# Attention's transfers on other queues, and the last combination ahead of the z gate

## The chip, the cores and the metric

The kernel runs on one core of a Trainium2 chip. Five engines work side by side, each in the order of its own instruction queue: TensorE (PE) multiplies matrices, VectorE (DVE), ScalarE (ACT) and GpSimd (POOL) work on tiles, and SyncE (SP) here only issues transfers. GpSimd issues transfers too. A transfer runs on the core's 16 DMA engines once its issuing queue has come to it and its waits are fulfilled. The metric is the time of one execution in device microseconds, the median over runs.

## The reference, cut to what matters

One step of a hybrid decoder with one layer: an input projection, an attention head group beside a state-space head group, an output projection, cross attention and an MLP. The change lies in the prompt's attention (2048 positions, 8 heads of 64): three dilated branches, whose outputs are averaged with the softmax of their log-sum-exps.

```python
DILATED_BRANCHES = ((128, 1), (512, 4), (2048, 16))

def combine_branches(outs, lses):
    w = jax.nn.softmax(jnp.stack(lses, axis=0), axis=0)
    return jnp.sum(w[..., None] * jnp.stack(outs, axis=0), axis=0)
```

Right behind it the kernel computes the other head group's gate, SiLU(z) times the scan's output, where z is a column block of the input projection.

## The kernel before

The prompt's attention is `phase_att`. It runs from about 655 to 963 us of the span. Its work is cut into four groups `g` of two heads, and each group into 24 steps: three branches `b`, eight pairs of query blocks each. A step issues the scores of its own pair (L975, TensorE), their masked maximum (L985, VectorE) and exponential (L987, ScalarE), the transposition of the pair before (L995, TensorE; L1000, VectorE), and the product with the values of the pair before that (L1008, TensorE). Then comes whatever has been put down for that step in the table `todo` by `at(step, function)`. So the order of the program is written out by hand: what a step's list says stands on the engines' queues behind the step's own instructions.

Put down there are:

- `first(g+1)`, at step 24g + 13: `load_qk` (L915) loads the next group's queries and keys, high and low parts, four transfers of 1 MB (L920), into the shared buffers `g_b` 0 to 3.
- `turned`, six casts per group on GpSimd (`by_residue`, L934), one per step from the group's first. They reorder queries and keys by residue for the second and third branches. The last two, `t_q`, read the queries' buffers again.
- `value`, the value loads (L941, L944, L947) on SyncE.
- `combine(g)` (L1020), which weighs and adds the three branch outputs of group g while the next group runs. `gather` collects maxima and sums by way of the array `s_stat` into `t_R`; `least` takes the least shift and the differences; `exps` the exponentials and the sum of the denominators; `coef` a reciprocal on VectorE (L1074) and a product (L1075), stores the coefficients to `s_coef` (L1076) and loads them back, broadcast over partitions, as `t_cf` (L1084). `chunk(c)`, four times, multiplies the outputs with them (L1093) and adds (L1096), on GpSimd; `store(c)` (L1103) writes the result to `s_att`. The tuple `times` (L1106) says how many steps into the next group each part stands; for the last group (g == 3) there is no next one, and the parts stand among the z gate's work.

For g == 3 the short operations run on VectorE, and each chunk has two multiplications and one addition on VectorE and one each on GpSimd.

The following stage, `Trunk.group`, is advanced step by step from attention's last steps by `next(fill)`. Its z gate takes the residual stream (L1383, loaded by GpSimd into `g_b` 0 to 7), multiplies it by the z columns (L1441, L1442, L1444), and in `gated` (L1571) evacuates each result: a product on VectorE (L1575), a tanh on ScalarE (L1576) and a product on GpSimd (L1577). `W.ahead` has GpSimd scale the next weights (L1274); ScalarE and VectorE split them into a high and a low part (L1230, L1231). The first two blocks of z are evacuated while attention's last steps end; the other two follow, and then the memory's keys, whose operand `load_memory` loads from GpSimd (L1629).

Of the kernel before, what the change touches and what calls it, by code (L numbers as in the profile page):

```python
# [10 lines left out]
F32 = mybir.dt.float32  # L11
# [7 lines left out]
P = 128  # L19
D = 1024  # L20
T = 2048
# [880 lines left out]
def phase_att(E, trunk):  # L902


    nc, tc = E.nc, E.tc
    with ExitStack() as ctx:
# [6 lines left out]
        s_att = E.s_att  # L913

        def load_qk(g):  # L915

            tiles = []
            for i, src in enumerate((E.s_qh, E.s_ql, E.s_kh, E.s_kl)):
                t = trunk.lend(i, T)
                nc.gpsimd.dma_start(t, src[g])  # L920
                tiles.append(t)
            return tiles

# [96 lines left out]
        def combine(g, stats, outs):  # L1020

            R = sp.tile([NS, 3, 2, P], F32, name="t_R", bufs=1)
            mn = sp.tile([NS, P], F32, name="t_mn", bufs=1)
            ex = sp.tile([NS, 3, P], F32, name="t_ex", bufs=1)
            dd = sp.tile([NS, 2, P], F32, name="t_dd", bufs=1)
            queue = nc.sync
            short = nc.vector if g == 3 else nc.gpsimd

            def nat(b, s):
                if b == 0:  # L1030
                    return R[:, 0, s, :]
                return R[:, b, s, :].rearrange("p (r a) -> p a r", r=4 if b == 1 else 16)

            def like(t, b):
                if b == 0:
                    return t
                return t.rearrange("p (a r) -> p a r", r=4 if b == 1 else 16)

            def gather():
                ps = pp.tile([P, 512], F32, name="t_pst", tag="t_pt", bufs=2)  # L1040
                for s in range(2):
                    for u in range(2):
                        nc.tensor.transpose(ps[:48, (2 * s + u) * P:(2 * s + u + 1) * P], stats[:, s, u, :], E.ident)
                rows = sp.tile([48, 4, P], F32, name="t_rows", bufs=1)
                nc.vector.tensor_copy(rows[:32].rearrange("p s l -> p (s l)"), ps[:32])
                for s in range(4):
                    nc.vector.tensor_copy(rows[32:48, s].rearrange("p (i j m) -> p i j m", i=4, j=4),
                                          ps[32:48, s * P:(s + 1) * P].rearrange("p (j i m) -> p i j m", i=4, j=4))
                dst = E.s_stat[g]
                nc.sync.dma_start(dst[0].rearrange("s r l -> r s l"), rows[0:16])  # L1050
                nc.sync.dma_start(dst[1].rearrange("s (i r) (q a) -> (r q) (s i) a", i=4, q=4),
                                  rows[16:32].rearrange("p s (i a) -> p (s i) a", i=4))
                nc.sync.dma_start(dst[2].rearrange("s i (r m) -> r (s i) m", m=8),
                                  rows[32:48].rearrange("p s (i m) -> p (s i) m", m=8))
                queue.dma_start(R.rearrange("p b s l -> p (b s) l"),
                                dst.rearrange("b (s u) r l -> (u r) (b s) l", s=2))

            def least():
                nc.vector.tensor_tensor(like(mn, 1), like(nat(0, 0), 1), nat(1, 0), op=ALU.min)
                nc.vector.tensor_tensor(like(mn, 2), like(mn, 2), nat(2, 0), op=ALU.min)  # L1060
                for b in range(3):
                    short.tensor_tensor(like(ex[:, b, :], b), like(mn, b), nat(b, 0), op=ALU.subtract)

            def exps():
                nc.scalar.activation(ex, ex, AF.Exp)
                short.tensor_tensor(dd[:, 0, :], ex[:, 0, :], nat(0, 1), op=ALU.mult)
                for b in (1, 2):
                    short.tensor_tensor(like(dd[:, 1, :], b), like(ex[:, b, :], b), nat(b, 1), op=ALU.mult)
                    short.tensor_tensor(dd[:, 0, :], dd[:, 0, :], dd[:, 1, :], op=ALU.add)

            cfs = {}

            def coef():
                nc.vector.reciprocal(dd[:, 0, :], dd[:, 0, :])  # L1074
                short.tensor_tensor(ex, ex, dd[:, 0:1, :].to_broadcast([NS, 3, P]), op=ALU.mult)  # L1075
                queue.dma_start(E.s_coef[g].rearrange("b (r l) -> r b l", l=P), ex)  # L1076
                for c in range(4 if g == 3 else 2):
                    bcast(c)

            def bcast(c):  # L1080
                cf = cfs[c] = sp.tile([P, 3, 512], F32, name="t_cf", tag="t_cf" if c < 2 or g < 3 else "t_o",
                                      bufs=2 if c < 2 or g < 3 else 5)
                for u in range(2):
                    queue.dma_start(cf[64 * u:64 * u + 64],  # L1084
                                    E.s_coef[g].rearrange("b (u t) -> u b t", u=2)[u, None, :, 512 * c:512 * c + 512]
                                    .to_broadcast([64, 3, 512]))

            def chunk(c):
                f = cfs[c].rearrange("p b (j l) -> p b j l", j=4)
                o = [outs[g, b].rearrange("p (j i l) -> p i j l", i=4, j=4)[:, c] for b in range(3)]  # L1090
                for b in range(3):
                    e = nc.vector if g == 3 and b < 2 else nc.gpsimd
                    e.tensor_tensor(o[b], o[b], f[:, b], op=ALU.mult)  # L1093
                for b in (0, 1):
                    e = nc.vector if g == 3 and b < 1 else nc.gpsimd
                    e.tensor_tensor(o[b + 1], o[b + 1], o[b], op=ALU.add)  # L1096
                if c < 2 and g < 3:
                    bcast(c + 2)
                if g == 3:
                    store(c)  # L1100

            def store(c):
                nc.sync.dma_start(s_att[g * P:(g + 1) * P, :T].rearrange("p (j i l) -> p i j l", i=4, j=4)[:, c],  # L1103
                                  outs[g, 2].rearrange("p (j i l) -> p i j l", i=4, j=4)[:, c])

            times = (0, 4, 4, 4, 6, 6, 7, 7) if g == 3 else (0, 3, 4, 5, 7, 8, 9, 10, 17, 17, 17, 17)  # L1106
            return zip(times, (gather, least, exps, coef, *(lambda c=c, f=f: f(c) for f in (chunk, store) for c in range(4))))

        steps = [(g, b, 2 * i) for g in range(4) for b in range(3) for i in range(8)]
        N = len(steps)  # L1110
        st16 = {}
        st, vs, stats, outs, ps, prs, ptb, todo, pos, end = {}, {}, {}, {}, {}, {}, {}, {}, {}, []
# [40 lines left out]
        def first(g):  # L1153
            st[g] = load_qk(g)
# [19 lines left out]
        for g in range(4):  # L1174
            if g < 3:
                at(24 * g + 13, lambda g=g: first(g + 1))
                at(24 * g + 15, lambda g=g: value(g + 1, 0))
                at(24 * g + 17, lambda g=g: value(g + 1, 1))
                at(24 * g + 26, lambda g=g: value(g + 1, 2))
            at(24 * g + 24, lambda g=g: [at(24 * g + 24 + d, f) for d, f in  # L1180
                                         combine(g, stats[g], outs)])
            for k in range(6):
                at(max(24 * g, 2) + k, lambda g=g, k=k: turned(g, k))
# [6 lines left out]
        i, fill = 0, trunk.work  # L1190
# [1190 lines left out]
```

## Time and profile before

| | |
|---|---|
| median of 3 runs | 3525.11 us (3522.56 to 3529.34) |
| profiled execution | 3526.22 us |
| its span | 3524.4 us |
| TensorE busy | 3318.4 us (94%) |
| VectorE, ScalarE, GpSimd busy | 57%, 33%, 37% |
| mean granted TensorE clock | 0.969 of full speed |

The span is what the profile covers of its execution, and each time below is counted from its start. In a timeline a row is a run of instructions of one line on one engine, with its start, its length, what it writes and reads, how many there were, and in brackets for how long the engine stood idle before it and what it then waited for. In a row of windows stand the stretch and its length, the busy time of each engine with the count of instructions, the granted TensorE clock (PEclk, 1.00 is full speed), the busy share of the DMA engines, and what they moved. Its share can come out above 1.

### The profile page before, as it was taken

The numbers are of one execution on the slowest core, as the hardware profiler recorded it, in microseconds if no ns is written. First come the engines' busy times: TensorE is split into PE (matmuls) and PEld (weight loads), VectorE is DVE, ScalarE is ACT, GpSimd is POOL, SyncE is SP. The second block draws the span as 40 slices with busy tenths as digits, with TensorE's granted clock in tenths as the row PEclk, the third lists the DMA queues.
The fourth block names the chain that finished last, engine by engine and source line by source line (L and its number), as shares of the span: only waits on it lengthen the run. The fifth ranks groups of instructions, "written<-read, shape, count | busy, mean of one in ns | idle before, by whom it ended". The sixth has DMA issues, their size and how long they took to land. (4 is left out here: it accounts for less than half of the span.)

```text
span 3524.4 us, 52948 instructions
## 1 busy us (share of the span) xinstructions
PE 3318.4 (94%) x20615; PEld 2945.5 (84%) x20615; DVE 2005.4 (57%) x4068; ACT 1145.6 (33%) x2604; POOL 1306.0 (37%) x1047
## 2 busy tenths in 40 slices
PE   9998988897978999999999999989999999999998
PEld 7998988676767887777776677789888999999998
DVE  4334889876665344567764455564334455555555
ACT  5433333586634333311111111243443311111113
POOL 1114455567633333586611122444224431122113
PEclk9999999898989999999999999999999999999999
DMA  7668333545675121355435533632441222222222
GB/s 207 204 201 237 88 96 94 187 122 161 166 193 145 56 62 40 117 198 195 163 102 183 163 109 98 208 103 61 137 130 33 90 96 78 96 94 92 96 79 97
DMA packets 406365, 447.25 MB, mean 127 GB/s; under 512 B 39868, under 2 KB 338543, under 8 KB 402530
## 3 DMA queue, kind: packets, MB, share of 16 engines
q1 hardware_dynamic: 376066, 382.51, 35.1%
q0 software_dynamic: 30048, 61.35, 6.0%
q8 instruction: 163, 2.67, 0.3%
q14 instruction: 88, 0.72, 0.1%
HBM read 368.33 MB, written 142.44 MB: 145 GB/s over the span
## 5 line engine op out<-in xcount | busy, mean ns | idle before, releaser
L1441 PE MATMUL g_g<-g_b,w_hi 128*128 128x352 f32 (+1 forms) x1760 | 629.5, 359 | 10.1 <-ACT w_hi L1230 8.7
L1442 PE MATMUL g_g<-g_b,w_lo 128*128 128x352 f32 (+1 forms) x1760 | 621.3, 354 | 8.2 <-DVE w_lo L1231 8.1
L1958 POOL TENSOR_TENSOR g_small<-g_small 128x352 f32<-128x352 f32 (+1 forms) x160 | 143.3, 897 | 960.6 <-ACT g_a L1957 960.6
L1231 DVE TENSOR_TENSOR w_lo<-w_raw,w_hi 128x512 fp32r<-128x512 f32 x400 | 345.6, 869 | 193.8 <-ACT w_hi L1230 193.0
L1230 ACT ACTIVATE w_hi<-w_raw 128x512 fp32r<-128x512 f32 x400 | 241.1, 622 | 610.6 <-issue 355.9
L1968 PE MATMUL g_a<-g_a,w_hi 128*128 128x352 f32 (+3 forms) x1076 | 391.3, 364 | 22.3 <-DVE g_a L1978 18.5
L1969 PE MATMUL g_a<-g_a,w_lo 128*128 128x352 f32 (+3 forms) x1076 | 384.8, 358 | 1.9 <-DVE w_lo L1231 1.9
L1970 PE MATMUL g_a<-g_a,w_hi 128*128 128x352 f32 (+3 forms) x1076 | 383.5, 356 | 0.9 <-DVE g_a L1959 0.9
L1441 PEld LDWEIGHTS g_g<-g_b,w_hi 128*128 128x128 f32 x1760 | 335.7, 191 | 56.7 <-ACT w_hi L1230 13.6
L1442 PEld LDWEIGHTS g_g<-g_b,w_lo 128*128 128x128 f32 x1760 | 335.3, 191 | 39.5 <-DVE w_lo L1231 9.9
L1444 PE MATMUL g_g<-g_b,w_hi 128*128 128x352 f32 (+1 forms) x1760 | 366.7, 350 | 0.0
L1978 DVE TENSOR_TENSOR g_a<-g_a,g_a 128x512 f32<-128x512 f32 (+2 forms) x504 | 292.4, 591 | 109.1 <-PE g_a L1970 108.0
L1444 PEld LDWEIGHTS g_g<-g_b,w_hi 128*128 128x128 f32 x1760 | 304.9, 188 | 30.5 <-DMA g_b<-s_xl 0.3
L1957 ACT ACTIVATE g_a<-g_small 128x352 fp32r<-128x352 f32 (+1 forms) x160 | 87.9, 551 | 634.8 <-DVE g_small L1956 634.8
L1956 DVE SCALAR_TENSOR_TENSOR g_small<-g_g,g_rb 128x352 f32<-128x352 f32 (+1 forms) x160 | 94.1, 588 | 316.6 <-PE g_g L1444 285.5
L1968 PEld LDWEIGHTS g_a<-g_a,w_hi 128*128 128x128 f32 x1076 | 202.7, 188 | 71.0 <-DVE g_a L1978 30.6
L1441 PE MATMUL g_g<-g_a,w_hi 128*128 128x352 f32 (+1 forms) x632 | 228.7, 363 | 5.7 <-ACT g_a L1510 4.2
L1442 PE MATMUL g_g<-g_a,w_lo 128*128 128x352 f32 (+1 forms) x632 | 226.3, 359 | 3.1 <-DVE w_lo L1231 2.9
L1970 PEld LDWEIGHTS g_a<-g_a,w_hi 128*128 128x128 f32 x1076 | 203.1, 189 | 23.7 <-DVE g_a L1959 1.3
L1969 PEld LDWEIGHTS g_a<-g_a,w_lo 128*128 128x128 f32 x1076 | 202.8, 188 | 22.5 <-DVE w_lo L1231 2.9
L987 ACT ACTIVATE w_spare<-w_spare,t_stats 128x256 f32<-128x256 f32 (+1 forms) x376 | 168.7, 450 | 74.5 <-DVE t_stats L985 74.3
L1959 DVE TENSOR_TENSOR g_a<-g_small,g_a 128x352 fp32r<-128x352 f32 (+1 forms) x160 | 186.4, 1166 | 2.6 <-POOL g_small L1958 2.4
(468 smaller groups left out, 6988.5 us busy)
## 6 DMA issues: line engine op xcount, KB each, us to landing
w_raw<-in_w_up_dram SPq DMA_DIRECT2D x64, 512.0 KB
w_raw<-in_w_down_dram SPq DMA_DIRECT2D x64, 512.0 KB
out_dram<-in_cache_win_k_dram SPq DMA_DIRECT2D x32, 1022.0 KB
out_dram<-in_cache_win_v_dram SPq DMA_DIRECT2D x32, 1022.0 KB
g_wide<-in_cache_win_k_dram SPq DMA_DIRECT2D x32, 512.0 KB
t_cf<-s_coef SPq DMA_DIRECT2D x32, 384.0 KB
g_spare<-in_cache_win_v_dram SPq DMA_DIRECT2D x48, 256.0 KB
a_xn<-in_x_prompt_dram SPq DMA_DIRECT2D x16, 512.0 KB
```

What stands on the lines that cost most here:

```text
L987: nc.scalar.activation(pr[:, u, :w], pr[:, u, :w], AF.Exp, bias=nm, scale=-1.0, accum_out=stats[:, 1, u, col:col + 1])
L1230: nc.scalar.activation(hi, src, AF.Copy)
L1231: nc.vector.tensor_tensor(lo, src, hi.bitcast(F32), op=ALU.subtract)
L1441: mm(ps[:, :n], hi[:, k], rhs[0][k][:, s], start=first and k == ks[0], stop=False)
L1442: mm(ps[:, :n], lo[:, k], rhs[0][k][:, s], start=False, stop=False)
L1444: mm(ps[:, :n], hi[:, k], rhs[1][k][:, s], start=False, stop=last and k == ks[-1])
L1958: nc.gpsimd.tensor_tensor(t1[:, :k], t1[:, :k], t1[:, :k], op=ALU.mult)
L1959: line.later(3, lambda: nc.vector.tensor_tensor(ul[:, s], t1[:, :k], uh[:, s].bitcast(F32), op=ALU.subtract))
L1968: mm(ps[:, :k], hi[:, j, c], us[f, j, 0][:, s], start=(j == 0), stop=False)
L1969: mm(ps[:, :k], lo[:, j, c], us[f, j, 0][:, s], start=False, stop=False)
L1970: mm(ps[:, :k], hi[:, j, c], us[f, j, 1][:, s], start=False, stop=(j == 1))
L1978: nc.vector.tensor_tensor(xs[m][:, s], xs[m][:, s], ps[:, :k], op=ALU.add)
```

## The change

The four loads of `load_qk` are issued by SyncE and no longer by GpSimd. The store of the coefficients and the loads of `t_cf` are issued by GpSimd and no longer by SyncE, and so are the last group's four stores to `s_att`. For the first three combinations `coef` and the chunks stand one step later; `least`, `exps` and the stores stay where they were. For the last combination `least`, `exps` and `coef` stand two steps earlier, ahead of the first evacuation of the z gate, and the chunks two steps earlier too; attention's last steps end with that, so that `load_memory` is put down one block earlier. From L1026 on, line numbers in the changed kernel are one lower.

```diff
@@ -917,7 +917,7 @@
             tiles = []
             for i, src in enumerate((E.s_qh, E.s_ql, E.s_kh, E.s_kl)):
                 t = trunk.lend(i, T)
-                nc.gpsimd.dma_start(t, src[g])
+                nc.sync.dma_start(t.bitcast(F32), src[g])
                 tiles.append(t)
             return tiles
 
@@ -1023,7 +1023,6 @@
             mn = sp.tile([NS, P], F32, name="t_mn", bufs=1)
             ex = sp.tile([NS, 3, P], F32, name="t_ex", bufs=1)
             dd = sp.tile([NS, 2, P], F32, name="t_dd", bufs=1)
-            queue = nc.sync
             short = nc.vector if g == 3 else nc.gpsimd
 
             def nat(b, s):
@@ -1052,7 +1051,7 @@
                                   rows[16:32].rearrange("p s (i a) -> p (s i) a", i=4))
                 nc.sync.dma_start(dst[2].rearrange("s i (r m) -> r (s i) m", m=8),
                                   rows[32:48].rearrange("p s (i m) -> p (s i) m", m=8))
-                queue.dma_start(R.rearrange("p b s l -> p (b s) l"),
+                nc.sync.dma_start(R.rearrange("p b s l -> p (b s) l"),
                                 dst.rearrange("b (s u) r l -> (u r) (b s) l", s=2))
 
             def least():
@@ -1073,7 +1072,7 @@
             def coef():
                 nc.vector.reciprocal(dd[:, 0, :], dd[:, 0, :])
                 short.tensor_tensor(ex, ex, dd[:, 0:1, :].to_broadcast([NS, 3, P]), op=ALU.mult)
-                queue.dma_start(E.s_coef[g].rearrange("b (r l) -> r b l", l=P), ex)
+                nc.gpsimd.dma_start(E.s_coef[g].rearrange("b (r l) -> r b l", l=P), ex)
                 for c in range(4 if g == 3 else 2):
                     bcast(c)
 
@@ -1081,9 +1080,9 @@
                 cf = cfs[c] = sp.tile([P, 3, 512], F32, name="t_cf", tag="t_cf" if c < 2 or g < 3 else "t_o",
                                       bufs=2 if c < 2 or g < 3 else 5)
                 for u in range(2):
-                    queue.dma_start(cf[64 * u:64 * u + 64],
-                                    E.s_coef[g].rearrange("b (u t) -> u b t", u=2)[u, None, :, 512 * c:512 * c + 512]
-                                    .to_broadcast([64, 3, 512]))
+                    nc.gpsimd.dma_start(cf[64 * u:64 * u + 64],
+                                        E.s_coef[g].rearrange("b (u t) -> u b t", u=2)[u, None, :, 512 * c:512 * c + 512]
+                                        .to_broadcast([64, 3, 512]))
 
             def chunk(c):
                 f = cfs[c].rearrange("p b (j l) -> p b j l", j=4)
@@ -1100,10 +1099,11 @@
                     store(c)
 
             def store(c):
-                nc.sync.dma_start(s_att[g * P:(g + 1) * P, :T].rearrange("p (j i l) -> p i j l", i=4, j=4)[:, c],
-                                  outs[g, 2].rearrange("p (j i l) -> p i j l", i=4, j=4)[:, c])
-
-            times = (0, 4, 4, 4, 6, 6, 7, 7) if g == 3 else (0, 3, 4, 5, 7, 8, 9, 10, 17, 17, 17, 17)
+                queue = nc.gpsimd if g == 3 else nc.sync
+                queue.dma_start(s_att[g * P:(g + 1) * P, :T].rearrange("p (j i l) -> p i j l", i=4, j=4)[:, c],
+                                outs[g, 2].rearrange("p (j i l) -> p i j l", i=4, j=4)[:, c])
+
+            times = (0, 2, 2, 2, 4, 4, 5, 5) if g == 3 else (0, 3, 4, 6, 8, 9, 10, 11, 17, 17, 17, 17)
             return zip(times, (gather, least, exps, coef, *(lambda c=c, f=f: f(c) for f in (chunk, store) for c in range(4))))
 
         steps = [(g, b, 2 * i) for g in range(4) for b in range(3) for i in range(8)]
```

SyncE, at the third group of attention, from the load of its third branch's values to the stores of the combination (`g_b` are the buffers of the next group's queries and keys, `t_v` value tiles). Rows with - stood there before, rows with + stand there now.

```order
 L947 DMA t_v<-s_v 128x2048
-L1076 DMA s_coef_88<-t_ex 32x3x128
-L1084 DMA t_cf<-s_coef_88 64x3x512 x8
+L920 DMA g_b_9688<-s_qh 128x2048
+L920 DMA g_b_9690<-s_ql 128x2048
+L920 DMA g_b_9692<-s_kh 128x2048
+L920 DMA g_b_9694<-s_kl 128x2048
 L941 DMA t_v_9788<-s_v 128x16x128
 L944 DMA t_v<-s_v 32x4x512 x4
 L1103 DMA s_att<-t_o 128x4x128 x4
```

The coefficients' nine transfers have left this place, and the four loads have taken it.

GpSimd at the same place, from the combination's last short product on, before:

```order
-L1075 TENSOR_TENSOR t_ex<-t_ex,t_dd 32x384
-L1093 TENSOR_TENSOR t_o<-t_o,t_cf 128x4x128 x3
-L1096 TENSOR_TENSOR t_o<-t_o 128x4x128 x2
-L1093 TENSOR_TENSOR t_o<-t_o,t_cf 128x4x128 x3
-L1096 TENSOR_TENSOR t_o<-t_o 128x4x128 x2
-L1093 TENSOR_TENSOR t_o<-t_o,t_cf 128x4x128 x3
-L1096 TENSOR_TENSOR t_o<-t_o 128x4x128 x2
-L1093 TENSOR_TENSOR t_o<-t_o,t_cf 128x4x128 x3
-L1096 TENSOR_TENSOR t_o<-t_o 128x4x128 x2
-L920 DMA g_b_9688<-s_qh 128x2048
-L920 DMA g_b_9690<-s_ql 128x2048
```

And now:

```order
+L1074 TENSOR_TENSOR t_ex<-t_ex,t_dd 32x384
+L1075 DMA s_coef_88<-t_ex 32x3x128
+L1083 DMA t_cf<-s_coef_88 64x3x512 x4
+L1092 TENSOR_TENSOR t_o<-t_o,t_cf 128x4x128 x3
+L1095 TENSOR_TENSOR t_o<-t_o 128x4x128 x2
+L1083 DMA t_cf<-s_coef_88 64x3x512 x2
+L1092 TENSOR_TENSOR t_o<-t_o,t_cf 128x4x128 x3
+L1095 TENSOR_TENSOR t_o<-t_o 128x4x128 x2
+L1083 DMA t_cf<-s_coef_88 64x3x512 x2
+L1092 TENSOR_TENSOR t_o<-t_o,t_cf 128x4x128 x3
+L1095 TENSOR_TENSOR t_o<-t_o 128x4x128 x2
```

The store of the coefficients and their first four loads stand between the product and chunk 0, two more loads behind chunk 0 and two behind chunk 1; the loads of queries and keys are gone from the chunks' end.

VectorE at the start of the z gate, before:

```order
L1567 TENSOR_SCALAR g_rbz<-g_rbz 128x1024
L1575 TENSOR_TENSOR g_small<-g_g,g_rbz 128x512
L1515 SCALAR_TENSOR_TENSOR g_a_11346<-g_small,g_a_11346 128x512
L1575 TENSOR_TENSOR g_small<-g_g,g_rbz 128x512
L1059 TENSOR_TENSOR t_mn<-t_R 32x128
L1060 TENSOR_TENSOR t_mn<-t_mn,t_R 32x128
L1062 TENSOR_TENSOR t_ex<-t_mn,t_R 32x128 x3
```

And now, from the reciprocal's product on (the rows of `least` and `exps` stand ahead of these, right behind L1567):

```order
L1074 TENSOR_TENSOR t_ex<-t_ex,t_dd 32x384
L1575 TENSOR_TENSOR g_small<-g_g,g_rbz 128x512
L1515 SCALAR_TENSOR_TENSOR g_a_11346<-g_small,g_a_11346 128x512
L1575 TENSOR_TENSOR g_small<-g_g,g_rbz 128x512
L1092 TENSOR_TENSOR t_o<-t_o,t_cf 128x4x128 x2
L1095 TENSOR_TENSOR t_o<-t_o 128x4x128
L1092 TENSOR_TENSOR t_o<-t_o,t_cf 128x4x128 x2
L1095 TENSOR_TENSOR t_o<-t_o 128x4x128
L1515 SCALAR_TENSOR_TENSOR g_a_11346<-g_small,g_a_11346 128x512
L1231 TENSOR_TENSOR w_lo<-w_raw,w_hi 128x512
```

The whole combination has moved ahead of the gate's first product (L1575), and chunks 0 and 1 (L1092, L1095) ahead of the low half of the next weights (L1231).

## Rows read from the trace of the kernel before

**Rows 1.** Windows of attention groups: length, busy time by engine, PEclk, DMA share, GB/s.
```profile
720.90:797.80 76.90, 67.67 (x762) 54.55 (x761) 56.21 (x255) 59.31 (x224) 52.95 (x39) 0.94 0.56 151
...
sum 229.10, PE 201.95 PEld 163.08 DVE 161.94 ACT 167.47 POOL 161.16; mean PE 67.32 PEld 54.36 DVE 53.98 ACT 55.82 POOL 53.72
```

**Rows 2.** Timeline of TensorE at two group starts: start, us, instruction, idle before.
```profile
797.80 0.48 PE L975 MATMUL t_pss<-g_b,g_b 64*128 64x128 f32 x2 [6.10 <-DMA g_b<-s_kh]
...
876.48 0.47 PE L975 MATMUL t_pss<-g_b,g_b 64*128 64x128 f32 x2 [7.07 <-DMA g_b<-s_kh]
```

**Rows 3.** Timeline of GpSimd, second group, same columns.
```profile
747.46 0.99 POOL L1075 TENSOR_TENSOR t_ex<-t_ex,t_dd 32x384 f32<-32x384 f32 x1
757.41 3.75 POOL L1093 TENSOR_TENSOR t_o<-t_o,t_cf 128x512 f32<-128x512 f32 x3 [8.96 <-DMA t_cf<-s_coef]
...
776.62 3.74 POOL L1093 TENSOR_TENSOR t_o<-t_o,t_cf 128x512 f32<-128x512 f32 x3 [0.22 <-DMA t_cf<-s_coef]
...
782.90 0.60 POOL L920 DMA_DIRECT2D g_b<-s_qh  x1
```

**Rows 4.** Timeline of VectorE, the reciprocal in the fourth group.
```profile
903.65 0.94 DVE L1074 RECIPROCAL t_dd<-t_dd 32x128 f32<-32x128 f32 x1 [4.07 <-POOL t_dd L1069]
```

**Rows 5.** Timeline of SyncE's queue, start of attention and second group.
```profile
640.56 0.37 SPq L577 DMA_DIRECT2D s_y<-s_yg  x1
...
730.17 0.39 SPq L947 DMA_DIRECT2D t_v<-s_v  x1
...
750.01 18.94 SPq L1084 DMA_DIRECT2D t_cf<-s_coef  x8
```

**Rows 6.** Windows of three stretches of transfers.
```profile
752.00:760.00 8.00, 8.00 (x86) 6.61 (x84) 4.33 (x24) 5.27 (x21) 2.58 (x3) 0.84 0.92 189
786.00:798.00 12.00, 5.90 (x72) 4.63 (x70) 5.12 (x31) 7.54 (x32) 6.52 (x2) 0.90 1.10 397
946.00:969.00 23.00, 19.25 (x137) 14.49 (x136) 10.33 (x43) 11.22 (x39) 5.48 (x11) 0.93 1.08 348
```

**Rows 7.** Timeline of TensorE, the first scores.
```profile
657.45 1.67 PE L975 MATMUL t_pss<-g_b,g_b 64*128 64x128 f32 x24
```

**Rows 8.** Timeline of GpSimd, third and fourth groups.
```profile
815.50 1.41 POOL L1062 TENSOR_TENSOR t_ex<-t_mn,t_R 32x128 f32<-32x128 f32 x3 [9.53 <-DVE t_mn L1060]
...
826.79 0.99 POOL L1075 TENSOR_TENSOR t_ex<-t_ex,t_dd 32x384 f32<-32x384 f32 x1
...
871.57 14.40 POOL L934 CAST g_b<-g_b 128x2048 fp32r<-128x2048 f32 x4 [6.83 <-DMA g_b<-s_qh]
885.95 1.89 POOL L1274 TENSOR_TENSOR w_raw<-w_raw,g_gm 128x1024 f32<-128x1024 f32 x1
...
917.65 3.76 POOL L1093 TENSOR_TENSOR t_o<-t_o,t_cf 128x512 f32<-128x512 f32 x3 [9.47 <-DMA t_cf<-s_coef]
...
944.00 0.60 POOL L1383 DMA_DIRECT2D g_b<-s_xh  x1
```

**Rows 9.** Timeline of TensorE, z gate and memory.
```profile
958.83 0.50 PE L1441 MATMUL g_g<-g_b,w_hi 128*128 128x512 f32 x1 [1.39 <-DMA g_b<-s_xh]
...
985.94 0.51 PE L1441 MATMUL g_g<-g_b,w_hi 128*128 128x512 f32 x1 [3.41 <-ACT w_hi L1230]
...
1030.38 0.58 PE L1223 MATMUL g_g<-g_kv,w_hi 128*128 128x256 f32 x1 [3.79 <-DMA g_kv<-s_ml]
```

**Rows 10.** Timeline of VectorE, combination of the last group.
```profile
979.99 0.37 DVE L1059 TENSOR_TENSOR t_mn<-t_R 32x128 f32<-32x128 f32 x1
...
987.51 0.55 DVE L1075 TENSOR_TENSOR t_ex<-t_ex,t_dd 32x384 f32<-32x384 f32 x1
```

**Rows 11.** Timeline of GpSimd, two chunks of the last group.
```profile
1000.40 1.73 POOL L1093 TENSOR_TENSOR t_o<-t_o,t_cf 128x512 f32<-128x512 f32 x1
...
1004.40 1.71 POOL L1093 TENSOR_TENSOR t_o<-t_o,t_cf 128x512 f32<-128x512 f32 x1
```

**Rows 12.** Window of a norm and a pass of the z gate.
```profile
1012.30:1020.00 7.70, 7.51 (x29) 5.11 (x28) 7.63 (x7) 4.85 (x7) 6.31 (x5) 1.00 0.12 35
```

## The prediction

> **What bounds the kernel now.** I read the windows by group first, then TensorE's waits in that stretch, then the timelines of GpSimd and SyncE around each wait. The reader is to see in the windows that the three groups of attention that follow the first take 229.1 us, and that in the first of them TensorE is busy for 67.67 us at a granted clock of 0.94 [rows 1]. That is 63.6 us at full clock; three times that is 191. So 38 us is all that can be won in this stretch: idle time, and the low clock that goes with it.
>
> The waits name the causes. Where a group ends, the first scores of the next wait for its keys, 6.10 and 7.07 us [rows 2]. In GpSimd's timeline the load of the next queries is issued at 782.90, right behind the last addition of the combination, whose first chunk began at 757.41 after 8.96 us of waiting for coefficients [rows 3]. The loads go when GpSimd comes to them, not when their buffers are free: GpSimd's last reader of them, the cast before 747.46, was done 35 us earlier. The combination's reciprocal, too, holds VectorE while it waits for GpSimd, 4.07 us at worst [rows 4].
>
> **Loads on SyncE.** In the new order the four loads stand behind a value load that was issued at 730.17 [rows 5], so SyncE is free when the buffers are, near 747 for group 2. Such loads ran at 397 GB/s when they were critical [rows 6]: 4.19 MB take 10.6 us and are there by about 760, while TensorE wants them near 790. Both transition waits go. For group 0 SyncE issues them behind a store at 640.56 [rows 5]; 10.6 us and some 2 to start make 653, and the first scores follow at 657.45 [rows 7]: hidden, with a risk of 0 to 3 us.
>
> What is late next is GpSimd itself, whose queue is one chain from group to group. Its four casts take 14.40, and from the subtractions at 815.50 to the end of the product at 827.78 it is busy throughout, 12.3 [rows 8]: 26.7 together. The four chunks take 25.5 (757.41 to 782.90) [rows 3]. Between the product's end and chunk 0 lies the wait for the coefficients; call it D, 9.0 us now. The sum is 61.2, just under TensorE's 63.6. The issues that SyncE gives up come on top.
>
> **Coefficients on GpSimd's queue.** Four more issues stand between the chunks, at 0.60 us each, as the issue at 782.90: 2.4 us per group. Chunk 2's coefficients are now issued behind chunk 0's additions and not behind its multiplications, some 2.6 us later; chunk 3's came 0.22 us after they were wanted even before [rows 3]. I take 0.8 us of new waiting per group, so 28.7 us for the chunks.
>
> D is the disputed term. The first coefficient loads went out at 750.01 [rows 5]; now they share the DMA engines with the q/k loads, which start at the same moment. From 752 to 760 the coefficients alone kept the engines 0.92 busy at only 189 GB/s, and the q/k loads filled them too, 1.10 [rows 6]. So nothing is spare: what one takes the other loses. The ends for D are 9.0 (the loads get out of the way; a little below, if they are through first) and 9.0 + 10.6 = 19.6 (the loads go entirely first). I take 14 in the two groups that load, the middle, since the rows show full engines on both sides and not which is served first; and 10 in the last, where no load starts: 9.47 before [rows 8], and one more issue. The sum is 38.
>
> The Trainium skill ("DMA: Bandwidth & Descriptors", Queues, rings and completion order) says that an engine alternates between the queues that have work, a packet at a time. By that neither waits for the whole of the other, so D would lie inside the ends; no run here shows the two together.
>
> The last chunk of group 2 then ends at 748.45 + 28.7 + 26.7 + 28.7 + 30.5 + 28.7 + 2.3 + 38 = 932.1. The 30.5 is 26.7 and two weight scalings of 1.89 [rows 8]; the 2.3 is four issues of residual loads that now stand ahead of the last chunk. It ended at 944.0 [rows 8], so 11.9 us earlier. TensorE by itself would be through its groups at about 720.9 + 191 = 912, so GpSimd decides. The reciprocal, one step later, no longer waits in group 1; in groups 2 and 3 it waits for a GpSimd that is late anyway, so this edit gains nothing of its own.
>
> **Where this reaches the end.** What TensorE waits for next is a residual load, until 958.83 [rows 9], 14.8 us after that chunk, among loads that run at 348 GB/s with the engines full [rows 6]. One more pair of them now goes out ahead of the last chunk: 1.05 MB, 3.0 us. The z gate's point moves by 11.9 + 3.0 = 14.9 us.
>
> **The combination of group 3 ahead of the evacuation.** On VectorE it runs from 979.99 to 988.06 [rows 10], 8.1 us, some of it slowed beside GpSimd; ahead of the gate's products I count 6.5, by which these come later. On GpSimd nine DMA issues (0.6 each, and 1.5 of waiting for the coefficients' store) now stand ahead of the gate's product and of the scaling of the next weights; on VectorE chunks 0 and 1 stand ahead of those weights' low halves. So the weights for which TensorE waited until 985.94 [rows 9] come 11 to 15 us later. Not all of it counts, since TensorE waited for the memory's load until 1030.38 anyway [rows 9]. GpSimd's work from there to the last scaling is four chunks at 4.0 [rows 11], four stores at 0.6, gate products and the scaling, so on the old clock that ends near 1017; the weights are split some 2.4 us later, and a pass of 6.2, a norm and a second pass (7.7 for the two, [rows 12]) end near 1033, with the memory there. I take +2.3 us. The ends are -2 (the chunks no longer collide with the gate) and +8 (of 11, only 3 hidden).
>
> **The sum.** -14.9 + 2.3 = -12.6 us on the profiled execution of 3526.2, which is 1.1 above the median of 3525.1: 3513.6, and 3512 (rounded down from 3512.5) against the median. Against no change, 0.2% is 7 us, about what a measurement can tell.
>
> **Rivals.** *The full gain.* D stays near 9.3, because the loads are issued in one go and half through when the coefficients come. The three D are 28, the tail costs nothing: -12.6 - 10 - 2.3 = -25, 3500; and if GpSimd isn't the bound at all, the whole 38, 3487. Against it stand the engine shares of 0.92 and 1.10.
>
> *A wash.* D is 18 in the two loading groups, 46 in all: -12.6 + 8 = -4.6, and with the tail at its upper end +1. About 3523. The waits for keys go, and GpSimd gives the time back while it waits for coefficients.
>
> *Slower.* The coefficient issues are themselves slow on GpSimd: 2 us each and not 0.6. Nine to a combination make 1.4 x 9 = 12.6 us, 38 over three groups, all on the engine that decides: -12.6 + 38 = +25, 3538, and more at the z gate. It decides from about 1.1 us an issue (12.6 / 27 = 0.47 on top). For it: these loads, 64 x 3 pieces each, never ran on GpSimd, so no row has their price there. Against: the issue at 782.90 with its 128 rows took 0.60 [rows 3].
>
> The Trainium skill ("SBUF — State Buffer", the box on "DVE blocks DMA") warns that GpSimd cannot write descriptors while VectorE runs certain copies within the on-chip memory. No row here shows such a stall; the price would be of the kind just given.
>
> **How the numbers follow.** Forecast 0.52, full gain 0.2, wash 0.15, slower 0.13. The forecast's own range is 3504 to 3521, from D between 12 and 16 and the tail's ends. The 8 in 10 go from 3492, inside the full gain, to 3527, past the wash. Faster by over 0.2%: most of the forecast and all of the full gain, 0.69. Within 0.2%: the wash and the forecast's upper edge, 0.18. Slower: 0.13.
>
> **What would show it.** Right: no wait for keys on TensorE behind the first group; q/k loads issued on SyncE near 747; chunk 0 starting 12 to 17 us behind the product in two groups and about 10 in the third; GpSimd idle only for D; the wait for a residual load still there, some 15 us earlier; the wait for the z gate's third block of weights longer, and the one for the memory's load gone. Wrong: D of 9 everywhere and a clock near 1.00 through the stretch (full gain), GpSimd idle for 18 us per group (wash), or issues of over 1.1 us there (slower).

## The result and the profile after

The changed kernel takes 3552.8 us (median of 4 runs, 3552.0 to 3554.2) against 3527.1 for the kernel before (median of 4 runs by now): ratio 1.0075, interval 1.0057 to 1.0092, slower by some 26 us. The forecast was 3512, its 8-in-10 range ended at 3527. The profiled execution took 3554.2 us, its span is 3552.4, 28.0 longer.

TensorE's waits in attention's last three groups and at the z gate, in the columns of a timeline:

```profile
798.41 1.63 PE L995 MATMUL t_pt<-ident,w_spare 128*128 128x128 f32 x4 [14.80 <-ACT w_spare L987]
883.28 1.63 PE L995 MATMUL t_pt<-ident,w_spare 128*128 128x128 f32 x4 [15.44 <-ACT w_spare L987]
961.50 1.63 PE L995 MATMUL t_pt<-ident,w_spare 128*128 128x128 f32 x4 [7.36 <-ACT w_spare L987]
973.86 0.50 PE L1441 MATMUL g_g<-g_b,w_hi 128*128 128x512 f32 x1 [0.99 <-DMA g_b<-s_xh]
1011.98 0.79 PE L1441 MATMUL g_g<-g_b,w_hi 128*128 128x512 f32 x1 [14.45 <-ACT w_hi L1230]
1020.51 0.79 PE L1442 MATMUL g_g<-g_b,w_lo 128*128 128x512 f32 x1 [7.73 <-DVE w_lo L1231]
1038.35 0.79 PE L1441 MATMUL g_g<-g_b,w_hi 128*128 128x512 f32 x1 [4.05 <-ACT w_hi L1230]
1056.87 0.41 PE L1222 MATMUL g_g<-g_kv,w_hi 128*128 128x256 f32 x1 [1.98 <-ACT w_hi L1230]
```

The waits for keys [rows 2] are gone, as forecast. In their place stand three waits that the prediction did not have, for ScalarE's exponentials near the end of each group. The z gate's point, the end of its last wait for a residual load, comes at 973.86, 15.0 us later than at 958.83 [rows 9]. Behind it the waits for weights are longer, so that the first of the memory's products, which in the kernel before was through its last wait at 1030.38 [rows 9], is through it at 1056.87. So the loss has two parts of like size: some 15 us up to that point, and 12 to 13 in the tail behind it.

What ScalarE waited for stands in its own timeline. First the kernel before, GpSimd's additions of the last chunk and ScalarE's copy next to them:

```profile
780.32 2.64 POOL L1096 TENSOR_TENSOR t_o<-t_o 128x512 f32<-128x512 f32 x2
...
784.55 1.03 ACT L1018 ACTIVATE t_o<-t_po 128x512 f32<-128x512 f32 x1
```

The same copy in the changed kernel, in two groups:

```profile
797.07 1.03 ACT L1018 ACTIVATE t_o<-t_po 128x512 f32<-128x512 f32 x1 [15.95 <-POOL t_o L1095]
...
881.94 1.03 ACT L1018 ACTIVATE t_o<-t_po 128x512 f32<-128x512 f32 x1 [16.59 <-POOL t_o L1095]
```

The branch outputs `t_o` have five buffers. A group writes three, so the third branch of a group gets the buffer of the first branch of the group before, and that one is read until the first addition of its last chunk. Before, that addition (the first of the two from 780.32) was through some 3 us ahead of the copy. Now it ends at 797.1, the copy waits 16 us, and the exponentials behind it on ScalarE wait with it, and TensorE for them.

Why the chunk is late, from GpSimd's timeline, the second group:

```profile
738.00 1.41 POOL L1061 TENSOR_TENSOR t_ex<-t_mn,t_R 32x128 f32<-32x128 f32 x3 [7.28 <-DVE t_mn L1059]
...
749.36 0.99 POOL L1074 TENSOR_TENSOR t_ex<-t_ex,t_dd 32x384 f32<-32x384 f32 x1
750.66 0.62 POOL L1075 DMA_DIRECT2D s_coef<-t_ex  x1 [0.30 <-POOL t_ex L1074]
756.60 2.46 POOL L1083 DMA_DIRECT2D t_cf<-s_coef  x4 [5.32 <-DMA s_coef<-t_ex]
767.78 3.75 POOL L1092 TENSOR_TENSOR t_o<-t_o,t_cf 128x512 f32<-128x512 f32 x3 [8.72 <-DMA t_cf<-s_coef]
...
792.12 3.70 POOL L1092 TENSOR_TENSOR t_o<-t_o,t_cf 128x512 f32<-128x512 f32 x3 [2.91 <-DMA t_cf<-s_coef]
...
798.33 3.78 POOL L934 CAST g_b<-g_b 128x2048 fp32r<-128x2048 f32 x1
```

The third and the fourth group, from their subtractions to chunk 0, and the end of the last chunk:

```profile
822.24 1.41 POOL L1061 TENSOR_TENSOR t_ex<-t_mn,t_R 32x128 f32<-32x128 f32 x3 [9.27 <-DVE t_mn L1059]
...
833.60 0.99 POOL L1074 TENSOR_TENSOR t_ex<-t_ex,t_dd 32x384 f32<-32x384 f32 x1
...
852.64 3.75 POOL L1092 TENSOR_TENSOR t_o<-t_o,t_cf 128x512 f32<-128x512 f32 x3 [9.43 <-DMA t_cf<-s_coef]
...
907.32 1.41 POOL L1061 TENSOR_TENSOR t_ex<-t_mn,t_R 32x128 f32<-32x128 f32 x3 [7.61 <-DVE t_mn L1059]
...
920.50 1.00 POOL L1074 TENSOR_TENSOR t_ex<-t_ex,t_dd 32x384 f32<-32x384 f32 x1
...
931.53 3.75 POOL L1092 TENSOR_TENSOR t_o<-t_o,t_cf 128x512 f32<-128x512 f32 x3 [5.11 <-DMA t_cf<-s_coef]
...
961.41 0.57 POOL L1383 DMA_DIRECT2D g_b<-s_xh  x1
```

From the product's end to chunk 0 it takes 17.4 and 18.1 us where a load runs beside it and 10.0 in the last group, where none does. The store of the coefficients alone takes over 5 us to land. SyncE issues the q/k loads just ahead of it (the first and the last of the four):

```profile
746.46 0.34 SPq L920 DMA_DIRECT2D g_b<-s_qh  x1
...
750.26 0.42 SPq L920 DMA_DIRECT2D g_b<-s_kl  x1
```

In windows of that stretch and of the last group's same stretch (length, busy time by engine, PEclk, DMA share, GB/s), the engines are full in the one and not in the other:

```profile
750.00:768.00 18.00, 18.00 (x213) 14.69 (x213) 14.63 (x67) 16.56 (x61) 3.66 (x7) 1.00 1.01 322
...
922.00:932.00 10.00, 10.00 (x121) 8.19 (x120) 8.26 (x40) 8.80 (x33) 3.31 (x6) 1.00 0.69 135
```

And the windows of two groups, from first scores to first scores: 83 and 85 us at a clock of 0.88 and 0.84. In the kernel before it was 75 and 79 us; its first scores stood at 722.41, 797.80 and 876.48, and the first window of [rows 1] begins 1.5 us ahead of them.

```profile
724.00:807.10 83.10, 67.29 (x745) 53.64 (x743) 54.94 (x247) 56.93 (x216) 57.98 (x45) 0.88 0.52 143
807.10:892.00 84.90, 68.92 (x745) 54.94 (x744) 54.82 (x245) 56.10 (x212) 57.08 (x45) 0.84 0.51 140
```

### The profile page after: what moved, and what is told of

Its sections match the earlier page's. It is cut to its first block, busy times and chain, and to the rows that moved or that the text cites. A ratio compares the mean times of both kernels' runs of the same rounds, so it can differ in the third digit from the quotient of the medians.

```text
span 3552.4 us, 52930 instructions
## 1 busy us (share of the span) xinstructions
PE 3321.6 (94%) x20615; PEld 2946.2 (83%) x20615; DVE 2010.8 (57%) x4068; ACT 1145.5 (32%) x2604; POOL 1318.5 (37%) x1071
## 5 line engine op out<-in xcount | busy, mean ns | idle before, releaser
L1231 DVE TENSOR_TENSOR w_lo<-w_raw,w_hi 128x512 fp32r<-128x512 f32 x400 | 355.2, 893 | 197.3 <-ACT w_hi L1230 196.8
L1442 PEld LDWEIGHTS g_g<-g_b,w_lo 128*128 128x128 f32 x1760 | 335.6, 191 | 42.4 <-DVE w_lo L1231 12.5
```

What stands on the lines that cost most here:

```text
L1231: nc.vector.tensor_tensor(lo, src, hi.bitcast(F32), op=ALU.subtract)
L1442: mm(ps[:, :n], lo[:, k], rhs[0][k][:, s], start=False, stop=False)
```

## The experiments

Theory A: GpSimd's last chunk frees the buffer into which ScalarE copies the third branch, and it is late because the coefficients and the q/k loads share the DMA engines and because GpSimd issues transfers between chunks. Theory B: the coefficients are slow on GpSimd's queue, whatever runs beside them. The tail was tested apart. Medians are of 5 to 10 runs, each against the kernel before on the same chip (3526.4 to 3528.3).

**Loads on SyncE alone (e1).**

```diff
-                nc.gpsimd.dma_start(t, src[g])
+                nc.sync.dma_start(t.bitcast(F32), src[g])
```

> Only the q/k loads move to SyncE; coefficients, times and tail as before. Theory A (GpSimd's last chunk frees the buffer into which ScalarE copies the third branch's output, and that chunk is late because coefficient and q/k transfers share the DMA engines): on SyncE the loads stand behind all eight coefficient loads and go out near 769, so the wait for coefficients stays at 9 us, ScalarE does not wait, the waits for keys (6.1 and 7.1 us) vanish and the z gate's point comes some 20 us earlier: 3507, 3500 to 3513. Theory B (the q/k loads are not the trouble, GpSimd's issuing of the coefficients is): the same 3507. Theory C (loads behind the coefficients on SyncE are late again): waits for keys of 3 us and more remain, 3520 to 3527.

Measured: 3507.7, ratio 0.9944 (0.9931 to 0.9957). With the coefficients still on SyncE, the loads stand behind them (SyncE's timeline):

```profile
752.31 19.38 SPq L1084 DMA_DIRECT2D t_cf<-s_coef  x8
771.73 0.60 SPq L920 DMA_DIRECT2D g_b<-s_qh  x1
```

So the wait for coefficients stays short (GpSimd's timeline):

```profile
759.61 3.75 POOL L1093 TENSOR_TENSOR t_o<-t_o,t_cf 128x512 f32<-128x512 f32 x3 [8.87 <-DMA t_cf<-s_coef]
```

In the groups no wait for keys or for ScalarE is left; the longest are the reciprocal's (2.1, 2.1 and 4.0 us). This part of the change by itself gains 19 us.

**Coefficients on GpSimd alone (e2)**, for the first three combinations, with the later step. The load of `t_R` stays on SyncE here and in e3, e4 and e8.

```diff
-            queue = nc.sync
+            queue = nc.sync if g == 3 else nc.gpsimd
-            times = (0, 4, 4, 4, 6, 6, 7, 7) if g == 3 else (0, 3, 4, 5, 7, 8, 9, 10, 17, 17, 17, 17)
+            times = (0, 4, 4, 4, 6, 6, 7, 7) if g == 3 else (0, 3, 4, 6, 8, 9, 10, 11, 17, 17, 17, 17)
```

> Only the coefficient transfers of the first three combinations move to GpSimd, with the reciprocal one step later; q/k loads stay on GpSimd behind the chunks, the tail as before. Theory A: no q/k load runs beside the coefficients, so the product's end to chunk 0 takes about 10 us in all three groups; issues and later coefficients of chunks 2 and 3 make the last chunk 4 to 5 us later, the loads behind it and the groups too: 3536 to 3542. Theory B: 17 to 18 us from product to chunk 0 as in the changed kernel, 3550 and more.

Measured: 3541.3, ratio 1.0046 (1.0032 to 1.0060). The first coefficients, with no load beside them:

```profile
748.55 0.62 POOL L1076 DMA_DIRECT2D s_coef<-t_ex  x1 [0.30 <-POOL t_ex L1075]
750.78 2.46 POOL L1084 DMA_DIRECT2D t_cf<-s_coef  x4 [1.61 <-DMA s_coef<-t_ex]
760.70 3.77 POOL L1093 TENSOR_TENSOR t_o<-t_o,t_cf 128x512 f32<-128x512 f32 x3 [7.45 <-issue]
```

12.5 us and 1.6 for the store, against 17.4 and 5.3: B is refuted. But the part costs 15 us even so: ScalarE waits for the last chunk here too (TensorE 9.8, 8.1 and 8.5 us), and the loads still follow that chunk. How much of the 15 belongs to the queue and how much to the later step was not run apart.

**The tail alone (e3)**: the last combination's times and queues as in the change, the rest as before.

```diff
-            queue = nc.sync
+            queue = nc.gpsimd if g == 3 else nc.sync
-            times = (0, 4, 4, 4, 6, 6, 7, 7) if g == 3 else (0, 3, 4, 5, 7, 8, 9, 10, 17, 17, 17, 17)
+            times = (0, 2, 2, 2, 4, 4, 5, 5) if g == 3 else (0, 3, 4, 5, 7, 8, 9, 10, 17, 17, 17, 17)
```

The stores of `store(c)` go by `queue` too.

> Only the last combination moves: its parts two steps earlier, its coefficient transfers and stores on GpSimd. If the z gate's late weights are the cost (TensorE waits 14.5, 7.7 and 4.1 us for them in the changed kernel, and the memory's first product comes 26.5 us later where the gate's point came 15.0 later): +9 to +13, 3536 to 3540. If that is hidden behind the memory's load, as the forecast had it: +2.3, 3529.

Measured: 3538.7, ratio 1.0032 (1.0020 to 1.0045): 12 us, not 2.3. TensorE waits 12.8, 7.1 and 4.4 us for weights, the last of these for a scaling that GpSimd begins behind its four chunks and stores (TensorE's rows and GpSimd's):

```profile
999.67 0.80 PE L1441 MATMUL g_g<-g_b,w_hi 128*128 128x512 f32 x1 [12.84 <-ACT w_hi L1230]
...
1022.82 1.91 POOL L1274 TENSOR_TENSOR w_raw<-w_raw,g_gm 128x1024 f32<-128x1024 f32 x1
...
1025.44 0.50 PE L1441 MATMUL g_g<-g_b,w_hi 128*128 128x512 f32 x1 [4.41 <-ACT w_hi L1230]
```

**All but the tail (e4)**: the edits of e1 and e2 together, which is the changed kernel with the last combination as before.

> The changed kernel with the last combination as before (times, queues and stores). Theory A: the waits of TensorE for ScalarE (14.8, 15.4 and 7.4 us) stay, the z gate's point some 15 us later than before, the tail's cost gone: 3538 to 3545. If the tail carries most of the loss: 3527 to 3533.

Measured: 3541.2, ratio 1.0042 (1.0029 to 1.0056). With e3 it adds up: 14.7 and 12.2 make 27, the whole 26. Within e4 the parts don't add: -19 (e1) and +15 (e2) would be -4.

**A sixth buffer (e5).** The changed kernel, with room from elsewhere:

```diff
-                                      bufs=2 if c < 2 or g < 3 else 5)
+                                      bufs=2 if c < 2 or g < 3 else 6)
-                    outs[g, b] = sp.tile([P, T], F32, name="t_o", bufs=5)
+                    outs[g, b] = sp.tile([P, T], F32, name="t_o", bufs=6)
-            ptb = sp.tile([P, 4, P], F32, name="t_ptb", bufs=4)
+            ptb = sp.tile([P, 4, P], F32, name="t_ptb", bufs=2)
-            mn = sp.tile([NS, P], F32, name="t_mn", bufs=1)
+            mn = dd[:, 1, :]
```

> The changed kernel with six buffers t_o for branch outputs where there were five (room from two t_ptb buffers fewer, and t_mn laid into t_dd). Theory A: ScalarE's copy of the third branch no longer waits for GpSimd's last chunk, TensorE's waits of 14.8, 15.4 and 7.4 us go. GpSimd's own chain remains, with 17 to 18 us for the coefficients: 12.3 + 17.7 + 30.5 + 14.6 = 75 us per group where the cycle was 84 to 85, so the last chunk of the third group ends near 945 and not 961: 3536, 3530 to 3542. If the buffer is not what holds ScalarE: 3550 and more, waits unchanged.

Measured: 3538.4, ratio 1.0031 (1.0019 to 1.0043). ScalarE's waits for the buffer are gone, and with them 14 of the 26 us. GpSimd now runs from group to group without a wait for VectorE's minimum, and its last chunk ends at 944 and not at 961 (its timeline):

```profile
812.38 1.40 POOL L1061 TENSOR_TENSOR t_ex<-t_dd,t_R 32x128 f32<-32x128 f32 x3
...
943.99 0.57 POOL L1383 DMA_DIRECT2D g_b<-s_xh  x1
```

What is late next is on SyncE: the stores of the results wait for the late chunks and hold the statistics of the next combination (SyncE's timeline, then VectorE's).

```profile
777.77 20.27 SPq L1103 DMA_DIRECT2D s_att<-t_o  x4
798.12 0.46 SPq L1049 DMA_DIRECT2D s_stat<-t_rows  x1
```

VectorE's minimum waits for them, and TensorE 8.2 us for VectorE:

```profile
803.60 1.52 DVE L1058 TENSOR_TENSOR t_dd<-t_R 32x128 f32<-32x128 f32 x1 [3.88 <-DMA t_R<-s_stat]
```

**The later step on top of e1 (e6)**: the diff of e1 and the two lines of `times` of e2.

> Loads on SyncE alone, and the reciprocal with what follows it one step later in the first three combinations. The reciprocal's stalls of TensorE (2.1, 2.1 and 4.0 us, with the low clock behind them some 17 us) go mostly. Theory A: the copy into the reused buffer comes 4 to 5 us earlier and then just meets the last chunk, 0 to 3 us of waiting per group: 3498, 3492 to 3503. If the step is worth nothing because the chunks come as much later: 3505 to 3509.

Measured: 3506.6, ratio 0.9948 (0.9936 to 0.9961): theory A's 3498 missed, the step is worth nothing. The reciprocal's stalls went down to 1.1 us, but ScalarE now meets the buffer (its waits: us in total, times, longest):

```profile
ACT t_o L1018 <- POOL t_o L1096: 12.1, 3, 5.5
```

**The tail's halves (e7, e8)**: of the diff of e3 only the two lines of `times`, and only the two of `queue`.

> The kernel before with only the last combination's times two steps earlier, its transfers on SyncE as before. If the order costs (combination and chunks 0 and 1 ahead of the gate's products and the low halves on VectorE): 3533 to 3538, with TensorE waiting 8 to 12 us for w_hi and some 8 for w_lo. If the nine issues on GpSimd cost: 3526 to 3529.

> The kernel before with only the last combination's coefficient transfers and stores on GpSimd, its times as before. If the order costs and not the queue: 3527 to 3531. If GpSimd's issues (9 at 0.6 us and 2 us of waiting ahead of the gate's product and the weights' scaling) carry the tail's 12 us: 3535 to 3539.

Measured: 3533.7, ratio 1.0023 (1.0013 to 1.0033), and 3534.5, ratio 1.0022 (1.0012 to 1.0032). The order costs what e7 expected of it, and the issues nearly what e8 expected: 7 to 8 us each. That makes 14.6 together where e3 has 12.2, a difference within the intervals. With the times, TensorE waits for the high half of the weights and then for the low one, which VectorE makes behind chunks 0 and 1:

```profile
990.01 0.79 PE L1441 MATMUL g_g<-g_b,w_hi 128*128 128x512 f32 x1 [6.73 <-ACT w_hi L1230]
1001.82 0.80 PE L1442 MATMUL g_g<-g_b,w_lo 128*128 128x512 f32 x1 [11.02 <-DVE w_lo L1231]
```

With the queues, GpSimd comes to the gate's product late, behind its eight loads, and VectorE's queue with it; one block later TensorE waits for weights:

```profile
1013.42 0.79 PE L1442 MATMUL g_g<-g_b,w_lo 128*128 128x512 f32 x1 [7.53 <-DVE w_lo L1231]
```

But that wait is not the one that ends last. GpSimd also comes 8.0 us later to the memory's load, and TensorE waits for that load as it did before. First the kernel before (GpSimd, then TensorE):

```profile
1019.88 1.57 POOL L1629 DMA_DIRECT2D g_kv<-s_mh  x2
...
1026.03 0.55 PE L1222 MATMUL g_g<-g_kv,w_hi 128*128 128x256 f32 x1 [6.22 <-DMA g_kv<-s_mh]
```

And e8:

```profile
1027.85 1.53 POOL L1629 DMA_DIRECT2D g_kv<-s_mh  x2
...
1033.08 0.55 PE L1222 MATMUL g_g<-g_kv,w_hi 128*128 128x256 f32 x1 [6.42 <-DMA g_kv<-s_mh]
```

So e7 pays through the weights, and e8 through the late load.

**Loads behind the coefficients (e10)**: the changed kernel, the loads on GpSimd behind the coefficient loads of chunk 3.

```diff
-                nc.sync.dma_start(t.bitcast(F32), src[g])
+                nc.gpsimd.dma_start(t, src[g])
-                at(24 * g + 13, lambda g=g: first(g + 1))
+                at(24 * g + 10, lambda g=g: first(g + 1))
```

> The changed kernel with the four loads on GpSimd behind the coefficient loads of chunk 3, so that no q/k load runs beside the first coefficients. If sharing the DMA engines costs the 17 to 18 us from product to chunk 0: 10 to 12.5 us in all three groups, the last chunks 3 to 4 us earlier after 2.3 us for the four issues, ScalarE's waits shorter by that: 3543, 3538 to 3548. If the coefficients' queue is slow by itself: 17 us stay, 3555 and more.

Measured: 3545.9, ratio 1.0047 (1.0034 to 1.0059), 7 us under the changed kernel (ratio 1.0075). The product's end lies 0.3 us ahead of the first row:

```profile
749.29 0.63 POOL L1075 DMA_DIRECT2D s_coef<-t_ex  x1 [0.30 <-POOL t_ex L1074]
751.52 2.46 POOL L1083 DMA_DIRECT2D t_cf<-s_coef  x4 [1.60 <-DMA s_coef<-t_ex]
760.58 3.76 POOL L1092 TENSOR_TENSOR t_o<-t_o,t_cf 128x512 f32<-128x512 f32 x3 [6.61 <-issue]
```

11.6 us, on the same queue (10.7 and 11.0 in the next two groups): the other 6 were the loads.

**Towards a better kernel (e9, e11, e12)**: e6 with the diff of e5, e1 with the diff of e5, and e9 with the first token group's residual loads on SyncE too:

```diff
-                E.nc.gpsimd.dma_start(t[:, s, :n], src[k * P:(k + 1) * P, cols])
+                if g == 0:
+                    E.nc.sync.dma_start(t[:, s, :n].bitcast(F32), src[k * P:(k + 1) * P, cols])
+                else:
+                    E.nc.gpsimd.dma_start(t[:, s, :n], src[k * P:(k + 1) * P, cols])
```

> Loads on SyncE, the coefficients on SyncE too, the reciprocal one step later in the first three combinations, and six buffers t_o. Theory A: the reciprocal's stalls go with the step, and ScalarE's waits that came in their place (up to 5.5 us per group with five buffers) go with the buffer; TensorE runs the three groups without a long wait at 63.6 to 65 us each: 3497, 3491 to 3502. If the step is worth nothing for another reason: 3505 to 3509.

> As e9, but with the reciprocal in its old step. The stalls of 2.1, 2.1 and 4.0 us and the low clock behind them stay, and ScalarE has no wait that the sixth buffer could take: 3507, as the loads on SyncE alone, 3502 to 3511.

> As e9, and the first token group's residual loads too go out on SyncE. In e9 TensorE still waits 3.2 and 1.8 us for residual loads at the z gate, behind GpSimd's last chunk. If GpSimd's queue sets them: four pairs go out some 15 us earlier, those waits go, 3499, 3494 to 3503. If the transfers themselves or the stores ahead of the other four pairs set them: 3502 to 3506.

Measured: 3504.1, ratio 0.9931 (0.9917 to 0.9944); 3504.7, ratio 0.9936 (0.9924 to 0.9949); 3498.8, ratio 0.9924 (0.9911 to 0.9938). All beat both kernels. e11 shows that the diff of e5 costs nothing on top of e1. e9 missed its 3497 and is no better than e11, so the later step gains nothing with six buffers either. ScalarE's waits are gone in e9, but TensorE still waits 3.7 and 3.1 us for VectorE in the groups, and then for residual loads, which GpSimd issues behind its last chunk (e9, TensorE's timeline).

```profile
936.57 0.50 PE L1441 MATMUL g_g<-g_b,w_hi 128*128 128x512 f32 x1 [3.16 <-DMA g_b<-s_xh]
939.15 0.80 PE L1441 MATMUL g_g<-g_b,w_hi 128*128 128x512 f32 x1 [1.81 <-DMA g_b<-s_xh]
```

In e12 one wait of 2.38 us is left of these. The intervals of e1, e6, e9, e11 and e12 overlap, so beyond e1 no single step is shown to gain.

## Why the prediction was wrong

- *The waits for keys go when SyncE issues the loads*: right, by the profile (the loads go out at 746.46, where 747 was forecast), and e1 shows what it is worth while the coefficients stay on SyncE, 19 us. With the coefficients on GpSimd it is worth nothing (e4 against e2). Attention's first scores came at 659.24, 1.8 us later than in [rows 7]; in e3, whose first loads go by GpSimd, they came at 661.47, so the loads need not be the cause.
- *D, from the product's end to chunk 0, is 14, 14 and 10*: too small; it was 17.4, 18.1 and 10.0, 45.5 and not 38. The reason given, engines full on both sides, was right (1.01 in the window; e10 and e2 give 11 to 12.5 without the loads), and the size lies near the upper end of its own bounds. The Trainium skill's rule of taking turns ("DMA: Bandwidth & Descriptors", Queues, rings and completion order) agrees with the trace in that the coefficients did not wait for the whole of the loads (by the prediction's sum 19.6), but they came close.
- *The last chunk of group 2 ends at 932*: the step that failed. It ended at 961.4, 29 us later, and the z gate's point came 15.0 us later where 14.9 earlier was forecast. Of these 7.5 are D, 1.9 the later start, some 2.6 the chunks, and 16.9 are idle time of GpSimd (9.27 and 7.61) for which the sum had no term. The same wait stood in [rows 8], 9.53 us at 815.50; the sum dropped it. The prediction let GpSimd run as a chain from group to group and let TensorE go ahead of it. But TensorE could not go ahead: its third branch needed the buffer that the last chunk frees. So the two form a loop: minimum on VectorE, GpSimd's products, coefficients, chunks, ScalarE's copy, the rest of the group, the next group's minimum. Its length is 84.2 and 85.1 us (738.00, 822.24 and 907.32, starts of the subtractions), against 63.6 of TensorE and 75 of GpSimd's own work and waits for coefficients (12.4 + 17.7 + 30.6 + 14.6, of the same rows and the casts). e5 cuts the loop: GpSimd's two waits go, its chunk ends at 944 with D as long as before (17.1, 19.0 and 9.9), and 14 us of the time go with them.
- *The reciprocal's later step gains nothing of its own*: right, but not for the reason given. With a GpSimd that is not late it gains nothing either: in e6 ScalarE meets the buffer, and with six buffers (e9 against e11) nothing is gained though those waits are gone. Why not was not run further.
- *The tail costs 2.3, at most 8*: too little; 12 (e3). That the first weights come 11 to 15 us later was right: 13.7 in e3 (999.67 against 985.94). What failed is how much of it hides. In e3, whose z gate's point lies where it did before (958.88), GpSimd's last scaling ended at 1024.7 where the sum had 1017: four chunks, four stores, two gate products and the scaling took 25.8 us from 998.92 on. TensorE began the memory's products at 1040.54, where the sum had them near 1033, and met late weights again there (2.00 and 0.96). So the weights outlasted the memory's load, for which nothing waits in e3 and in the changed kernel.
- *The rivals*: "slower" was forecast at 3538 through slow issues at 2 us; the issues took 0.58 to 0.67, about as in [rows 3]. The "wash", with D at 18, had D right and put the tail at +8 where it cost 12, but shares the missing loop.

## What to carry to other kernels

Before an engine's queue is made longer, list the buffers that its last instruction frees and who takes them next: an engine with 37% busy time can close a loop with the one that is the bound. A transfer that is moved ahead by 36 us lands among others: the q/k loads beside the small coefficient transfers cost 6 to 7 us per combination, behind them nothing that the wait for coefficients shows (8.9 in e1, as before; e10). And a chain's sum needs a term for every arrow back to the engine that feeds it, or it is only a lower bound.

## What the runs showed of the hardware

A small store and its reload are hit hard by big transfers that start beside them: the 48 KB store of coefficients took about 5.3 us to land beside the q/k loads and 1.6 without (changed kernel, e2), and the first coefficient loads 11.2 and 11.9 us from the first issue to use in two groups, against 9.1 and 8.2 in the same groups of e10 and 9.9 and 8.6 in e2, though the engines moved 322 GB/s in all. The coefficients' issues on GpSimd took 0.58 to 0.67 us each, where the q/k loads' took 0.54 to 0.62 in the kernel before, and the result stores 0.79 to 0.82.
